# Float32r scores over stacked rows for the forgetting attention, with its forget sums moved into masks that GpSimd builds

## The chip, the cores and the metric

The kernel runs on one core of one Trainium2 chip. The metric is the device time of one execution in microseconds; the kernel before took 1037.12 us (median of 3 runs, 1036.83 to 1037.17). Engines are named as in the profile: PE is TensorE (PEld its weight loads), DVE is VectorE, ACT is ScalarE, POOL is GpSimd, SP is SyncE, which issues most of the DMAs. An engine works through its own instructions in the order in which they were written; they meet other engines through semaphores.

## What is computed

Two layers of a decoder trunk on 256 tokens of width 1024, all in float32. A layer is a half-step SwiGLU, a mixer and a second half-step SwiGLU, each behind an RMSNorm and added to the trunk. The mixer makes one projection `u @ w_in` and splits it into three groups of heads of width 64: A (4 query heads, one shared key head, keys chosen by a top-k indexer), B (4 heads, with 256 tokens plain causal attention), and C, the forgetting attention that the change is about:

```python
cq = rms_norm(cq, c_q_norm);  ck = rms_norm(ck, c_k_norm)          # 8 heads
log_f = log_sigmoid(cf + forget_bias);  c = cumsum(log_f)          # one value per token and head
s = einsum('bqhd,bkhd->bhqk', q, k) * D ** -0.5
s = s + c[query] - c[key]                                          # forget sums
s = where(key <= query, s, -inf);  p = softmax(s)
o_c = (p @ v) * sigmoid(cg)
h = h + concat(o_A, o_B, o_C) @ w_out
```

## The kernel before

**Tiling.** Tokens are two halves of 128 (`t` = 0, 1). Weights stream in as raw tiles of up to 1 MB (`Weights`, lines 57 to 139; SP issues the loads, five raw buffers). Each unit of 128 x 1024 numbers is split into a high part in float32r (a cast on ScalarE, line 118) and a low part (a subtraction on VectorE, line 122), and products are made of three float32r matmuls, high x high, high x low, low x high (`mm3`, line 305). `W.pump()` splits one more unit; it may run up to seven units ahead of the one in use, and the low part of a unit is made one pump after its high part. All matmuls but transposes go through `mm` (line 302), so they all stand at line 303 in the profile. A plain float32 matmul shows as two instructions there, a float32r one as one.

**The mixer's order.** `mixer` (line 660) walks the eight column groups of the projection in the order of `CHUNKS` (iq, ib, b, a, ck, cq, cv, cg), with four units each: 32 steps. After a step `run_side` (line 667) emits what `at_step(n, fn)` has put down for it, and then a pump follows. When a group is complete its `post_...` function takes the result out of PSUM. The side work that matters here: `log_sigmoid` at step 27; `cumsum` at step 29 (line 869), which sums the forget gates over tokens with two small matmuls and writes `c` and `-c`; `c_norm` at step 25 (line 977), which computes the RMS factors of the C queries and keys and scales both on GpSimd; `amask` at step 32; and `post_cg` after it (line 990), which makes the output gate `sg` of group C on ScalarE and VectorE.

**C queries and keys.** `cqa[t]` and `cka[t]` (lines 293 and 294) hold 8 heads of 66 columns: 64 of the head, then `c` and 1 for the queries, 1 and `-c` for the keys. So a product over 66 rows gives the score with the forget sums in it. `c_T(j)` (line 1135) turns two heads: four transposes of the queries, four of the keys, one copy on ScalarE, one on VectorE. `scores` (line 1004) then makes the C scores with two plain float32 matmuls a head (lines 1010 and 1011). Heads of A and B instead go through `products` (line 743): the query rows are stacked, 64 high over 64 low (`stack`, line 713), the keys stand twice, and two float32r matmuls, with the keys' high part and with their low part, do the work of a float32 one.

**The head loop** (lines 1149 to 1182) runs the 4 A heads and 8 C heads two at a time, in six blocks, software-pipelined. Block k emits: `flip` of the pair 2k, 2k+1 (transposes of the exponentials, line 1034), `outT` of the pair before (line 1064), `scores` of the next pair (one fused VectorE instruction for each half adds the mask, negates and takes the row minimum, line 1023), their exponentials (`exps`, line 1027), `c_T(k)` while k < 4, `values` of the pair (line 1043), and one or two halves of the output projection (`out_halves`, line 1120), whose every second half carries a pump. Ahead of the loop stand the scores and exponentials of the first pair and two halves. PSUM has four banks for the tag "gu", which all of these use in turn.

## Time and profile before

| | |
|---|---|
| median of 3 runs | 1037.12 us (1036.83 to 1037.17) |
| the profiled execution | 1037.25 us |
| its span, first to last instruction | 1035.5 us |
| granted TensorE clock | 1.000 |
| moved by DMA | 181.61 MB, mean 175 GB/s |

The prediction quotes views of the profile of that one execution. Shares of busy time by engine are an average over the span. The chain that ended last follows the work back from the last instruction: at each step to what released it. The timeline lists instructions in order of time; behind an instruction stands, in brackets, the idle time of its engine before it and what ended it. Groups by line give output, inputs, shapes, count, then busy time in us, mean ns of one, and the engine's idle time before them. A row of the DMA issues gives the size in KB and the median time from issue to landing in us. Ends of matmuls are modelled by the profiler, so a row's own length is longer than the distance from one matmul to the next.

### The profile page before, as it was taken

The page shows a single profiled execution, that of the slowest core. Times are in us where ns is not written, and L with a number is a line of the kernel's source. Part 1 is how long each engine was busy: PE and PEld are TensorE (multiplying, and loading weights), DVE is VectorE, ACT ScalarE, POOL GpSimd, SP SyncE. Part 2 cuts the span into 40 slices and gives each one's busy share as a digit, 9 for nine tenths or more (in the row PEclk, how much of TensorE's full clock was granted, in tenths as well). Part 3 has the DMA queues.
Part 4 walks back from the last instruction along what each step waited for, and adds up shares of the span by engine and source line. Part 5 has one row for each costly group of instructions (what it writes and reads, how often), then busy time and mean ns, then how long its engine had stood idle before and what let it go on. Part 6 is the DMA issues. An engine that isn't in the chain of part 4 may idle for free.

```text
span 1035.5 us, 15082 instructions
## 1 busy us (share of the span) xinstructions
PE 1031.3 (100%) x5641; PEld 898.4 (87%) x5641; DVE 808.0 (78%) x1537; ACT 592.1 (57%) x1045; POOL 147.3 (14%) x177
## 2 busy tenths in 40 slices
PE   9999999999999999999999999999999999999998
PEld 8888888898888888888888888888988988888887
DVE  6977778789876877777788777787898768777776
ACT  6655556666854655555465555557676646555552
POOL 2003000167800000000000110002766000000000
PEclk9999999999999999999999999999999999999999
DMA  9664656554431364645645564664455224564631
GB/s 324 224 240 162 208 188 198 182 191 170 158 127 42 123 230 150 230 168 203 198 163 193 182 224 146 241 186 172 164 195 170 83 69 160 180 204 162 236 130 41
DMA packets 130808, 181.61 MB, mean 175 GB/s; under 512 B 7040, under 2 KB 104624, under 8 KB 130736
## 3 DMA queue, kind: packets, MB, share of 16 engines
q1 hardware_dynamic: 130704, 180.66, 51.3%
q8 instruction: 44, 0.72, 0.3%
q14 instruction: 28, 0.23, 0.1%
q10 hardware_dynamic: 32, 0.01, 0.0%
HBM read 179.60 MB, written 1.05 MB: 174 GB/s over the span
## 4 chain that ended last, share of the span: by engine, by line
PE 100%; DVE 0%; POOL 0%; issue 0%; POOLq 0%
PE ps_gu L303 66%; PE ps_acc L303 30%; PE ps_acc L338 1%; PE ps_gu L1037 1%; PE ps_gu L1140 1%; PE ps_acc L738 0%; PE ps_acc L1037 0%; PE ps_gu L1070 0%; PE ps_acc L495 0%; PE ps_acc L364 0%; PE ps_acc L1070 0%; PE ps_gu L179 0%; DVE trunk L377 0%; POOL ones L183 0%; POOL minus_half L185 0%
## 5 line engine op out<-in xcount | busy, mean ns | idle before, releaser
L122 DVE TENSOR_TENSOR wl<-raw,wh 128x1024 fp32r<-128x1024 f32 (+2 forms) x342 | 417.0, 1225 | 24.7 <-ACT wh L118 24.7
L118 ACT CAST wh<-raw 128x1024 fp32r<-128x1024 f32 (+2 forms) x341 | 343.1, 1036 | 5.4 <-PE ps_gu L303 4.8
L303 PE MATMUL ps_gu<-xhl,wh 128*128 128x512 f32 x1408 | 330.2, 390 | 0.0
L303 PEld LDWEIGHTS ps_gu<-xhl,wh 128*128 128x128 f32 x1408 | 262.7, 188 | 53.8 <-ACT wh L118 0.3
L303 PEld LDWEIGHTS ps_gu<-xhl,wl 128*128 128x128 f32 x1408 | 176.0, 191 | 4.3 <-issue 0.2
L303 PE MATMUL ps_gu<-xhl,wl 128*128 128x256 f32 x1408 | 179.2, 283 | 0.1
L303 PE MATMUL ps_gu<-wh,xhl 128*128 128x512 f32 (+2 forms) x512 | 157.2, 377 | 0.0
L442 DVE TENSOR_TENSOR tmp<-ps_gu,tmp 128x256 f32<-128x256 f32 x176 | 73.0, 423 | 107.8 <-ACT tmp L441 107.5
L303 PE MATMUL ps_acc<-wh,hh 128*128 128x512 f32 (+1 forms) x352 | 137.2, 390 | 0.0
L303 PE MATMUL ps_acc<-wl,hh 128*128 128x512 f32 (+1 forms) x352 | 137.0, 389 | 0.0
L303 PE MATMUL ps_acc<-wh,hl 128*128 128x512 f32 (+1 forms) x352 | 136.5, 388 | 0.0
L441 ACT COPY tmp<-ps_gu 128x256 f32<-128x256 f32 x176 | 63.5, 371 | 93.5 <-PE ps_gu L303 93.2
L303 PEld LDWEIGHTS ps_gu<-wh,xhl 128*128 128x128 f32 x512 | 94.8, 188 | 14.6
L456 ACT CAST hh<-tmp 128x256 fp32r<-128x256 f32 x80 | 32.6, 407 | 119.7 <-DVE tmp L453 119.7
L303 PE MATMUL ps_gu<-wl,xhl 128*128 128x512 f32 (+2 forms) x256 | 95.7, 374 | 0.0
L448 ACT ACTIVATE tmp<-tmp 128x256 f32<-128x256 f32 x88 | 36.9, 419 | 82.3 <-DVE tmp L446 81.9
L314 POOL TENSOR_TENSOR y_n<-msq,minus_half 128x2 f32<-128x2 f32 x6 | 6.8, 1141 | 530.9 <-DVE msq L313 530.9
L303 PEld LDWEIGHTS ps_acc<-wh,hl 128*128 128x128 f32 x352 | 66.1, 188 | 13.9
L303 PEld LDWEIGHTS ps_acc<-wh,hh 128*128 128x128 f32 x352 | 66.2, 188 | 12.6
L303 PEld LDWEIGHTS ps_acc<-wl,hh 128*128 128x128 f32 x352 | 66.2, 188 | 12.2
L303 PEld LDWEIGHTS ps_gu<-wl,xhl 128*128 128x128 f32 x256 | 48.2, 188 | 6.7
L327 ACT ACTIVATE xhl<-ps_acc,gT 128x256 fp32r<-128x256 f32 x48 | 19.1, 474 | 38.7 <-PE ps_acc L338 35.6
(221 smaller groups left out, 1000.4 us busy)
## 6 DMA issues: line engine op xcount, KB each, us to landing
raw<-in_ffn_w_down_dram SPq DMA_DIRECT2D x44, 1024.0 KB, 4.9
raw<-in_ffn_w_gate_dram SPq DMA_DIRECT2D x42, 1024.0 KB, 6.6
raw<-in_ffn_w_up_dram SPq DMA_DIRECT2D x42, 1024.0 KB, 7.3
raw<-in_w_in_dram SPq DMA_DIRECT2D x24, 1024.0 KB, 4.9
raw<-in_w_out_dram SPq DMA_DIRECT2D x8, 1024.0 KB, 4.9
raw<-in_w_in_dram SPq DMA_DIRECT2D x4, 768.0 KB, 4.9
raw<-in_w_in_dram SPq DMA_DIRECT2D x4, 656.0 KB, 3.9
raw<-in_ffn_w_gate_dram SPq DMA_DIRECT2D x3, 512.0 KB, 7.0
```

Source lines behind the costliest of these rows:

```text
L118: self.nc.scalar.copy(hv, src)
L122: (engine or self.nc.vector).tensor_tensor(lv, self.srcs[self.n_low], hv.bitcast(F32), op=ALU.subtract)
L303: T.matmul(o, l, r, start=start, stop=stop, skip_group_check=True)
L314: G.tensor_tensor(y, dst, minus_half[:, :n], op=ALU.pow)
L327: A.activation(self.h[:, m], src, AF.Copy, scale=gT[:, self.col + m:self.col + m + 1])
L338: T.transpose(ps[:, i, t * P:(t + 1) * P], trunk[:, t, (2 * mp + i) * P:(2 * mp + i + 1) * P], ident)
L441: A.copy(o, ps[:, 1])
L442: V.tensor_tensor(o, ps[:, 0], o, op=ALU.add)
L448: A.activation(th, t_, AF.Tanh, scale=0.5)
L456: (V.tensor_copy if late else A.copy)(hh, t_)
L1037: T.transpose(b[:, j * P:(j + 1) * P], pj[i][:, j * P:(j + 1) * P], ident)
L1140: T.transpose(b[:66, i * S + t * P:i * S + (t + 1) * P], src[t][:, 2 * hp_ + i, :], ident)
```

## The change

The C heads get the form of A and B, and the forget sums leave the product.

- `cq` and `ck` (64 columns a head) take the place of `cqa` and `cka`; the memsets of their ones go. `c_norm` scales the queries only.
- `cumsum` keeps one copy of `c`. `turn_sums` (step 30) transposes `c` to rows by head with two transposes, negates it on ScalarE, and writes it to a scratch tensor in DRAM from ScalarE's queue; `load_sums` (step 31) reads it back from the same queue, broadcast over all 128 partitions (1 MB), into `minus_c`.
- `c_parts(j)` makes the stacked queries of two heads (high copy on ScalarE, low subtraction on GpSimd) and the doubled, scaled keys (two multiplications on GpSimd). Those of pairs 0 and 1 stand at step 31, those of pairs 2 and 3 at the end of blocks 1 and 2.
- `decay(j)` builds the masks of two heads on GpSimd in four additions: `-c[key]` + `c[query]` + causal mask. It stands ahead of the loop for pair 0 and at the end of blocks 0 to 2 for the others.
- `c_T(j)` turns queries with four float32r matmuls against the identity and keys with four transposes, then copies both on ScalarE; the keys' low part, a subtraction on VectorE (`key_low`), comes after the values of the block. The two buffers of `cT` alternate.
- The C scores go through `products`, and the fused VectorE instruction reads the head's mask.
- In the loop `exps(2k+2)` stands ahead of `c_T(k)` and `exps(2k+3)` behind it.

```diff
@@ cumsum, in post_ib
-                for t in range(2):
-                    c = b[:, 8 * t:8 * t + 8]
-                    A.copy(cqa[t][:, :, 64], c)
-                    A.activation(cka[t][:, :, 65], c, AF.Copy, scale=-1.0)
+                st["c"] = sm.tile([P, 2, 8], F32, name="c", tag="c", bufs=1)
+                A.copy(st["c"].rearrange("p t h -> p (t h)"), b[:, 0:16])
+
+            def turn_sums():
+                b = bank("acc")
+                for t in range(2):
+                    T.transpose(b[:8, t * P:(t + 1) * P], st["c"][:, t], ident)
+                n = tmp(S)[:8]
+                A.activation(n, b[:8, :S], AF.Copy, scale=-1.0)
+                st["row"] = dram.tile([8, S], F32, name="minus_c_row", tag="minus_c_row")
+                nc.scalar.dma_start(st["row"], n)
+
+            def load_sums():
+                d = st["row"]
+                st["minus_c"] = at.tile([P, 8, S], F32, name="minus_c", tag="kT")
+                nc.scalar.dma_start(st["minus_c"], bass.AP(tensor=d.tensor, offset=d.offset,
+                                                           ap=[[0, P], [S, 8], [1, S]]))
 
             at_step(SUMS_STEP, cumsum)
+            at_step(SUMS_STEP + 1, turn_sums)
+            at_step(SUMS_STEP + 2, load_sums)
@@ new functions
+        def c_parts(j):
+            hs2 = slice(2 * j, 2 * j + 2)
+            q = tp.tile([P, 512], F32R, name="stacked", tag="tmp")
+            q4 = q.rearrange("p (t h s d) -> p t h s d", t=2, h=2, s=2)
+            A.copy(q4[:, :, :, 0], cq[:, :, hs2])
+            G.tensor_tensor(q4[:, :, :, 1], cq[:, :, hs2], q4[:, :, :, 0].bitcast(F32), op=ALU.subtract)
+            k = tmp(512)
+            k4 = k.rearrange("p (t h s d) -> p t h s d", t=2, h=2, s=2)
+            for t in range(2):
+                G.tensor_tensor(k4[:, t], ck[:, t, hs2, None, :].to_broadcast([P, 2, 2, HD]),
+                                st["rk"][:, 8 * t + 2 * j:8 * t + 2 * j + 2, None, None].to_broadcast([P, 2, 2, HD]),
+                                op=ALU.mult)
+            beside[j] = [x.rearrange("p (t h c) -> p t h c", t=2, h=2) for x in (q, k)]
+
+        def decay(j):
+            m = st["minus_c"][:, 2 * j:2 * j + 2]
+            c = st["c"][:, :, 2 * j:2 * j + 2, None]
+            first = at.tile([P, 2, P], F32, name="first", tag="first", bufs=2)
+            tri2 = causal[:, None, 0:P].to_broadcast([P, 2, P])
+            G.tensor_tensor(first, m[:, :, 0:P], c[:, 0].to_broadcast([P, 2, P]), op=ALU.add)
+            G.tensor_tensor(first, first, tri2, op=ALU.add)
+            G.tensor_tensor(m, m, c[:, 1].to_broadcast([P, 2, S]), op=ALU.add)
+            G.tensor_tensor(m[:, :, P:S], m[:, :, P:S], tri2, op=ALU.add)
+            for i in range(2):
+                decays[2 * j + i] = first[:, i], m[:, i]
@@ c_norm, in post_cq
                 rs = head_rs(c_ss.rearrange("p i t h -> p (i t h)"), 32, "c")
-                for t in range(2):
-                    for i, d in enumerate((cka, cqa)):
-                        x = d[t][:, :, 0:64]
-                        scale_heads(x, x, rs[:, 16 * i + 8 * t:16 * i + 8 * t + 8])
+                st["rk"] = rs[:, 0:16]
+                for t in range(2):
+                    scale_heads(cq[:, t], cq[:, t], rs[:, 16 + 8 * t:24 + 8 * t])
 
             at_step(25, c_norm)
+            at_step(31, lambda: c_parts(0))
+            at_step(31, lambda: c_parts(1))
@@ scores
+                products(b[:, 0:P], q[:, 0:P], [c[:, 0:P] for c in k], True, True)
+                products(b[:, P:3 * P], q[:, P:S], [c[:, 0:S] for c in k], False, True)
                 if kind == "C":
-                    mm(b[:, 0:P], q[:, 0:P], k[:, 0:P], True, True)
-                    mm(b[:, P:3 * P], q[:, P:S], k[:, 0:S], False, True)
+                    masks = decays.pop(h)
...
-                    V.tensor_tensor_reduce(s[:, c], b[:, c], mask[:, c], scale, 3e38, op0=ALU.add, op1=ALU.min,
+                    V.tensor_tensor_reduce(s[:, c], b[:, c], masks[t], scale, 3e38, op0=ALU.add, op1=ALU.min,
@@ c_T
+        cT = xp.tile([P, 2, 4, 2, S], F32R, name="cT", tag="xhl")
+
+        def c_T(j):
+            q, k = beside.pop(j)
+            d = cT[:, j % 2]
+            bq, bk = bank("gu"), bank("gu")
+            for i in range(2):
+                for t in range(2):
+                    mm(bq[:, i * S + t * P:i * S + (t + 1) * P], q[:, t, i], identr, i + t == 0, True)
+            for i in range(2):
+                for t in range(2):
+                    T.transpose(bk[:, i * S + t * P:i * S + (t + 1) * P], k[:, t, i], ident)
+            bq, bk = (b.rearrange("p (h s) -> p h s", h=2) for b in (bq, bk))
+            A.copy(d[:, 0], bq)
+            A.copy(d[:, 1], bk)
+
+            def key_low():
+                V.tensor_tensor(d[:, 2], bk, d[:, 1].bitcast(F32), op=ALU.subtract)
+
+            return key_low
@@ the head loop
+        decay(0)
         two(0, scores, exps)
...
                 scores(2 * k + 3)
-                two(k + 1, exps)
+                exps(2 * k + 2)
             if k < 4:
-                c_T(k)
+                key_low = c_T(k)
             if not last:
+                exps(2 * k + 3)
                 two(k, values)
+            if k < 4:
+                key_low()
+            if 0 < k < 3:
+                c_parts(k + 1)
+            if k < 3:
+                decay(k + 1)
             for _ in range(HALVES[k]):
                 next(halves)
```

More of the change, by code (lines that the diff above doesn't have):

```diff
@@ L292 @@
     identr = cp.tile([P, P], F32R, name="identr")
-    cqa = [at.tile([P, 8, 66], F32, name=f"cqa{t}", tag=f"cqa{t}") for t in range(2)]
-    cka = [at.tile([P, 8, 66], F32, name=f"cka{t}", tag=f"cka{t}") for t in range(2)]
+    cq = at.tile([P, 2, 8, HD], F32, name="cq", tag="cq")
+    ck = at.tile([P, 2, 8, HD], F32, name="ck", tag="ck")
     va = [at.tile([P, 13, 65], F32, name=f"va{t}", tag=f"va{t}") for t in range(2)]
     for t in range(2):
-        G.memset(cqa[t][:, :, 65:66], 1.0)
-        G.memset(cka[t][:, :, 64:65], 1.0)
         G.memset(va[t][:, :, 64:65], 1.0)
@@ L958, in c_sums @@
             for t in range(2):
-                evac(dst[t][:, :, 0:64], heads(ps[t], 8), t)
+                evac(dst[:, t], heads(ps[t], 8), t)
                 sq.append(squares(ps[t], t, 8))
@@ L968, in post_ck @@
         def post_ck(ps):
-            c_sums(0, cka, ps, 21)
+            c_sums(0, ck, ps, 21)
         def post_cq(ps):
-            c_sums(1, cqa, ps, 25)
+            c_sums(1, cq, ps, 25)
             for t in range(2):
-                q = cqa[t][:, :, 0:64]
+                q = cq[:, t]
                 G.tensor_tensor(q, q, gc[:, None, :].to_broadcast([P, 8, HD]), op=ALU.mult)
@@ L1130, in mixer @@
         halves = out_halves()
-        c_both = xp.tile([P, 2, 8, S], F32, name="cT", tag="xhl")
-        cT = [c_both[:, 0], c_both[:, 1]]
-        def c_T(hp_):
-            for d, src in zip(cT, (cqa, cka)):
-                b = bank("gu")
-                for i in range(2):
-                    for t in range(2):
-                        T.transpose(b[:66, i * S + t * P:i * S + (t + 1) * P], src[t][:, 2 * hp_ + i, :], ident)
-                (A.copy if src is cqa else V.tensor_copy)(d[:66, 2 * hp_:2 * hp_ + 2],
-                                                         b[:66].rearrange("p (a b) -> p a b", a=2))
+        cT = xp.tile([P, 2, 4, 2, S], F32R, name="cT", tag="xhl")
[15 more added lines that the diff above has]
+            return key_low
         def qk_ac(kind, h):
```

10 lines of the change are left out of this document (6 added, 4 removed).

## The prediction

> **What bounds the kernel now.** I read the page's first part (busy time by engine) and its fourth (the chain that ended last, shares by engine) first.
>
> ```profile
> PE 1031.3 (100%) x5641; PEld 898.4 (87%) x5641; DVE 808.0 (78%) x1537; ACT 592.1 (57%) x1045; POOL 147.3 (14%) x177
> ```
>
> ```profile
> PE 100%; DVE 0%; POOL 0%; issue 0%; POOLq 0%
> ```
>
> TensorE is busy for the whole span and the chain never leaves it. So whatever TensorE no longer issues is saved one for one, and whatever makes it wait is lost one for one; the other engines count only where they make it wait. The stage of the change is the attention of each layer. Next I read the chain in order of time there (layer 0: start, length, what, count of instructions).
>
> ```profile
> 280.90 9.22 PE ps_gu L303 x44
> 290.12 2.77 PE ps_acc L303 x12
> 292.89 0.77 PE ps_gu L1037 x6
> 293.66 0.92 PE ps_gu L303 x8
> 294.58 0.87 PE ps_gu L1140 x8
> 295.45 1.29 PE ps_gu L303 x12
> 296.74 1.45 PE ps_acc L303 x6
> 298.19 0.66 PE ps_gu L1037 x6
> 298.85 0.22 PE ps_gu L1070 x2
> 299.06 1.31 PE ps_gu L303 x8
> 300.38 0.87 PE ps_gu L1140 x8
> ```
>
> The first row is steps 30, 31 and 32 (36 projection matmuls) and the scores of two A heads (8 instructions); with 0.92 for the scores, as in the fourth row, a step is (9.22 - 0.92) / 3 = 2.77 us, and the steps end at 283.67, 286.43 and 289.20. Then comes one `out_halves` pair, and at 292.89 block 0 of the head loop: flips, scores of two A heads, `c_T(0)`, values, one half. Block 1 starts at 298.19, and 299.06 is its scores of two C heads. There is no gap in the loop, but the first flips take 0.77 against 0.66 in block 1: there TensorE already waits for the first exponentials, so the entry of the loop has no slack. Blocks 2 and 3 have flips, outT, C scores, `c_T`, values and one half: 0.66 + 0.22 + 1.31 + 0.87 + 1.29 + 1.45 = 5.80 us.
>
> **The change, TensorE first.** C scores: a plain float32 pair (K = 66) takes 1.31 us, a float32r pair over 128 rows, which A is already, 0.92. That is -0.39 for each of 4 pairs in 2 layers: **-3.1 us**. A float32r matmul after float32 work can pay for the switch: six matmuls of a half take 1.45 behind the values, twelve 2.77 behind float32r scores, so 1.45 - 2.77 / 2 = 0.07. The A scores at 293.66 show nothing of it behind flips. Bounds 0 to 0.07 for each C pair, I take 0.05: **+0.4**. `c_T` keeps 8 instructions; the four that turn the queries are now float32r matmuls with the identity, at most 0.92 / 8 = 0.115 each as in the A scores, against 0.87 / 8 = 0.109: +0.02 a pair, **+0.2**. `turn_sums` adds two transposes (0.66 / 6 = 0.11 each) and one more return to float32r (0.07): 0.3 a layer, **+0.6**. The cumsum matmuls stay. TensorE alone: **-1.9 us**, bounds -2.7 (no switch, no dearer query) to -1.8.
>
> **The entry of the loop.** ScalarE and VectorE over steps 30 to 32 (timeline: start, length, what, idle before and its releaser):
>
> ```profile
> 283.80 1.05 ACT L118 CAST wh<-raw 128x1024 fp32r<-128x1024 f32 x1 [0.60 <-PE ps_gu L303]
> 286.52 1.06 ACT L118 CAST wh<-raw 128x1024 fp32r<-128x1024 f32 x1 [1.67 <-PE ps_gu L303]
> 289.52 1.27 ACT L995 ACTIVATE sg<-ps_gu,hr 128x512 f32<-128x512 f32 x2 [1.94 <-DVE hr L992]
> ```
>
> ```profile
> 288.13 1.22 DVE L122 TENSOR_TENSOR wl<-raw,wh 128x1024 fp32r<-128x1024 f32 x1
> 289.27 0.16 DVE L992 TENSOR_SCALAR hr<-y_n 128x2 f32<-128x2 f32 x1
> ```
>
> These chains feed the first exponentials: high part of a weight unit (ScalarE) - its low part (VectorE, 288.13) - `hr` - the gate `sg` (ScalarE) - two gate operations, score rows (VectorE) - exponentials - flips. Prices of what is put in, from the groups by line, from the start of the execution (an issue on ScalarE's queue) and from the DMA issues (size, us to landing):
>
> ```profile
> L1141 DVE COPY cT<-ps_gu 66x512 f32<-66x512 f32 x8 | 5.5, 684 | 0.0
> ```
>
> ```profile
> L1141 ACT COPY cT<-ps_gu 66x512 f32<-66x512 f32 x8 | 4.5, 561 | 0.0
> ```
>
> ```profile
> L741 DVE TENSOR_TENSOR bkT<-ps_acc,bkT 128x512 fp32r<-128x512 f32 x4 | 2.6, 677 | 0.0
> ```
>
> ```profile
> L740 ACT CAST bkT<-ps_acc 128x512 fp32r<-128x512 f32 x4 | 2.2, 615 | 0.0
> ```
>
> ```profile
> L717 ACT CAST stacked<-bqr 128x256 fp32r<-128x256 f32 x4 | 1.5, 464 | 0.0
> ```
>
> ```profile
> 0.78 0.46 ACTq L175 DMA_DIRECT2D tmp<-in_ffn_norm_dram  x1
> ```
>
> ```profile
> raw<-in_w_in_dram SPq DMA_DIRECT2D x24, 1024.0 KB, 4.9
> ...
> out_dram<-trunk SPq DMA_DIRECT2D x2, 128.0 KB, 1.8
> ...
> gb<-in_c_k_norm_dram SPq DMA_DIRECT2D x2, 32.0 KB, 8.1
> ...
> tmp<-in_ffn_norm_dram ACTq DMA_DIRECT2D x1, 8.0 KB, 2.5
> ```
>
> At step 30 ScalarE must wait for the transposes (283.67 + 0.22, and about 0.2 to be seen), negate (no row; bounds 0.2 to 0.46 between a short activation and L717, I take 0.4), and issue the write: 284.5. Its high part of step 30 runs to about 286.0. At step 31 the load stands in ScalarE's queue and waits until the write has landed; the smallest write of the trace takes 1.8, the 8 KB transfer on this queue 2.5: 286.3 to 287.0, and 0.46 for the issue (nothing, if ScalarE does not stand still for it): about 286.8 to 287.5. **Queued behind that waiting load** are the two copies of `c_parts(0)` and `(1)` (0.46 each at most), the high parts of steps 31 and 32, then the gate. The high part of step 31, which ran at 283.80, starts at 287.5 to 288.4. Its low part stood at 288.13 and now starts at 288.6 to 289.5, 0.5 to 1.4 later; 0.3 of that is TensorE's own delay. So the gate loses 0.2 to 1.1, or nothing if the issue is free and the write quicker than any row; I take 0.4.
>
> On VectorE there is a second cost. Two low parts while GpSimd scales C keys and queries, two without it, and GpSimd's own side at the first place (timeline):
>
> ```profile
> 276.76 4.05 DVE L122 TENSOR_TENSOR wl<-raw,wh 128x1024 fp32r<-128x1024 f32 x2
> ```
>
> ```profile
> 282.62 2.35 DVE L122 TENSOR_TENSOR wl<-raw,wh 128x1024 fp32r<-128x1024 f32 x2
> ```
>
> ```profile
> 276.70 1.05 POOL L690 TENSOR_TENSOR cqa<-cqa,y_c 128x512 f32<-128x512 f32 x1
> 277.70 2.03 POOL L690 TENSOR_TENSOR cka<-cka,y_c 128x512 f32<-128x512 f32 x1
> ```
>
> So a low part beside GpSimd operations costs (4.05 - 2.35) / 2 = 0.85 more, and the GpSimd one up to 1.0 more (2.03 against 1.05). From about 287.3 GpSimd now runs six operations of `c_parts`, where it had nothing to do before; the low part of step 31 falls among them: 0 to 0.85, I take 0.6. Together **+1.0 a layer, +2.0 us**; bounds 0 to 2.0 a layer. It meets the flips with no cover.
>
> [...]
>
> **The loop.** The last exponential of block 1 and the last of its values on VectorE (timeline), and GpSimd's groups of 256 elements, slow and fast:
>
> ```profile
> 301.46 0.49 ACT L1031 ACTIVATE p<-tmp,nm 128x256 f32<-128x256 f32 x1
> ```
>
> ```profile
> 302.78 0.29 DVE L1062 TENSOR_TENSOR o<-ps_gu,ri 128x128 f32<-128x128 f32 x1
> ```
>
> ```profile
> L684 POOL TENSOR_TENSOR bkr<-bkr,tab 128x256 f32<-128x256 f32 x4 | 5.0, 1256 | 0.3
> ...
> L684 POOL TENSOR_TENSOR aqr<-aqr,tab 128x256 f32<-128x256 f32 x4 | 3.1, 765 | 0.3
> ```
>
> VectorE gives up a copy (0.68) and takes up a subtraction (0.68), moved behind the values: nothing, as long as it ends before the next block's second flip, which reuses that bank. In block 1 the values end at 302.54 on TensorE (298.19 and the five pieces behind it) and at 303.07 on VectorE, 0.53 later; with two C heads a little more, 0.7. So in a block of 5.4 (5.80 - 0.39) they end at 4.0 and 4.7, the subtraction at 5.4, and the flip comes at 5.4 + 0.33 = 5.75: cover 0.3. ScalarE gives up 0.56 and takes up 2 x 0.62 and 0.46, 1.1 us a block; the second head's exponentials come some 1.2 later, and their flip is at 5.75 while they end before 5: hidden. Masks: the row operation only reads another tile, nothing.
>
> GpSimd: 256 elements cost 0.77 in the fast group, 512 cost 1.05, so `c_parts` is 3 x 0.77 = 2.3 and `decay` 3 x 0.77 + 1.05 = 3.35. The 1 MB of negated sums is issued near 287 and lands after 4.9 (a weight load) to 8.1 (the slowest broadcast), 292 to 295; `decay(0)` ends by 298.5. The first C row needs scores that start at 299.06, and some 1.5 later after the entry's loss: hidden. The narrow place is `c_parts(3)`: its copy follows the last exponentials of block 2. In block 1 those ended at 301.95, 3.76 after its start; with two copies ahead of them it is 5.0 (3.76 + 1.24), with its own copy about 5.3 (copies in a row overlap a little). GpSimd's three operations then end at 5.3 + 2.3 = 7.6, and a low part among them makes it 8.4. The keys are turned in block 3 at 5.45 + 0.66 + 0.22 + 0.92 + 0.46 = 7.7. Between nothing and 0.7, I take 0.5; with 0.1 for a low part beside `decay(0)` that delays score rows in block 0, **+0.6 a layer, +1.2 us**. `c_parts(2)` has block 1's second half of weights as cover (1.4).
>
> What else moves costs nothing, with this cover: `c_norm` drops two scalings and `cumsum` three small copies, ahead of units that ScalarE splits several steps before TensorE uses them; the memsets stood at the start; weight loads on SP's queue wait for low parts that are at most 1 us later, with up to five loads under way; the extra 1 MB a layer stands beside 181 MB. Without that cover each would cost no more than its own 0.2 to 1 us.
>
> Sum: -1.9 + 2.0 + 1.2 = **+1.3 us**. The profiled execution took 1037.25 (span 1035.5 and 1.75 around it), 0.13 above the median of the runs: 1038.55 there, **1038.4** as a median.
>
> **The rivals.**
> - *GpSimd becomes the bound (slower).* Place: `c_parts(3)` and `decay(3)`. If 256 elements cost L684's mean of 1.26 rather than 0.77, and 512 cost 1.5 (between 1.05 and 2.03), `c_parts` is 3.8 and `decay` 5.3. `c_parts(3)` then ends at 5.3 + 3.8 = 9.1, 1.4 late, and `decay(3)` 5.3 after that, 14.4, where the score rows of block 4 want it at 2 x 5.45 + 1.7 + 1.4 = 14.0: 1.4 and 0.4 are 1.8 a layer instead of 0.5. It decides from about 0.9 per 256 elements (3 x 0.9 + 5.3 = 8.0). Time 1041; with every operation at its contended worst (1.8 and 2.0), past 1050. For: the group's mean. [...]
> - [...] If each of the low part and the two gate operations waits for a whole GpSimd operation (0.77 to 0.85), the entry costs 0.4 + 2.3 = 2.7 rather than 1.0: +3.4, so 1041.8; halfway 1040. [...]
> - *Everything is hidden (faster).* If the write is quicker than any row, ScalarE does not stand still for an issue and GpSimd's operations miss the low parts, only TensorE's -1.9 is left (-2.7 to -1.8): 1035.2, 1034.4 to 1035.3. Against: the entry already waits, 0.77 against 0.66.
> - *The sums land late.* They would have to take 11 us (287 to 298); the slowest row is 8.1. Small, and inside the first rival. That float32r over 128 rows does not run at 0.92 a pair is excluded by the A rows.
>
> **How the numbers follow.** A run of this kernel can be told from no change at about 0.2%, 2.07 us: 1035.05 and 1039.2. Forecast, up to 1039.2: 0.46. All hidden: 0.16, half of it under 1035.05. GpSimd the bound: 0.23. The port at the gate: 0.15. So faster 0.08, same 0.46 + 0.08 = 0.54, slower 0.38. The range 1035.0 to 1042.5 leaves out about 0.07 below and 0.12 above; the forecast's own is 1036.3 to 1039.2.
>
> **What would show it.** C pairs of 8 instructions in 0.92 to 1.0 in the chain; two transposes of the sums and a `DMA` wait on ScalarE between steps 30 and 31; the gate 0.5 to 1.5 later behind the projection's end and first flips of more than 0.77 or a wait ahead of them; GpSimd near 0.77 per 256 elements; a wait ahead of the key transposes of block 3 alone. I am wrong if ScalarE passes step 31 without a wait, if TensorE waits for GpSimd in blocks 1, 2 or 4, or if low parts beside GpSimd keep 1.22.

## The result, and the profile after

The changed kernel takes 1043.56 us (median of 6 executions, 1041.04 to 1047.07) against 1037.03 (median of 6, 1036.83 to 1037.42) for the kernel before: a ratio of 1.0064, with a 95% interval of 1.0053 to 1.0076. It is slower by 0.64%, above the range of the prediction. The six times stand in two groups: 1041.0 to 1041.9 with a granted TensorE clock of 0.999 to 1.000 over the whole span, and 1045.2 to 1047.1 with 0.995. So there are two things to explain. The profiled execution took 1041.46 us and belongs to the first group; its span is 1039.4 us, 3.9 more than before, and 2.06 us lie around it instead of 1.75.

The busy time by engine and the chain that ended last, from the page of the changed kernel:

```profile
PE 1030.8 (99%) x5645; PEld 896.8 (86%) x5645; DVE 812.9 (78%) x1537; ACT 598.2 (58%) x1057; POOL 191.9 (18%) x225
```

```profile
PE 97%; DVE 2%; DMA 0%; ACT 0%; issue 0%; POOL 0%; SPq 0%; ACTq 0%
```

TensorE is busy for 0.5 us less than before and yet the span is longer: 97% of the chain is TensorE's and 2% is VectorE's, where it was 100%. So TensorE waits somewhere. The waits of TensorE (engine, line, for what; us in total, times, longest):

```profile
PE ps_gu L1084 <- ACT p L1077: 2.8, 2, 2.1
PE ps_gu L302 <- POOL minus_half L186: 1.0, 1, 1.0
PE ps_gu L1084 <- ACT p L1078: 0.4, 2, 0.2
...
PE ps_gu L302 <- DVE pT L1086: 0.3, 1, 0.3
```

The second row stands at the start of the program and was there before as well. L1084 is `flip`: the first flips of the head loop wait for the first exponentials, 2.1 us in layer 0 and 0.6 in layer 1. To see why the exponentials are late, follow VectorE's row of operations. First before (timeline; start, length, what), then after, both in layer 0:

```profile
287.19 0.23 DVE L858 TENSOR_SCALAR amask<-score 128x128 f32<-128x128 f32 x1
287.33 0.49 DVE L860 SCALAR_TENSOR_TENSOR amask<-score,cst 128x128 f32<-128x128 f32 x2
287.86 0.36 DVE L862 TENSOR_SCALAR amask<-amask 128x384 f32<-128x384 f32 x1
```

```profile
284.59 0.61 DVE L850 MAX8 m<-score 128x8 f32<-128x128 f32 x2
...
285.77 1.22 DVE L122 TENSOR_TENSOR wl<-raw,wh 128x1024 fp32r<-128x1024 f32 x1
286.91 0.77 DVE L857 TENSOR_SCALAR amask<-score 128x128 f32<-128x128 f32 x1
287.60 1.33 DVE L859 SCALAR_TENSOR_TENSOR amask<-score,cst 128x128 f32<-128x128 f32 x2
288.96 0.78 DVE L861 TENSOR_SCALAR amask<-amask 128x384 f32<-128x384 f32 x1
289.67 1.63 DVE L122 TENSOR_TENSOR wl<-raw,wh 128x1024 fp32r<-128x1024 f32 x1
291.22 0.58 DVE L1039 TENSOR_SCALAR hr<-y_n 128x2 f32<-128x2 f32 x1
```

From the mask on (L857) every operation has grown by 0.4 us or more, whatever its size: the two of L859 went from 0.49 to 1.33 together, and `hr`, which works on 2 columns, from 0.16 to 0.58. GpSimd's operations in that stretch, in layer 0 and in layer 1 of the changed kernel:

```profile
286.30 1.29 POOL L979 TENSOR_TENSOR stacked<-cq,stacked 128x256 fp32r<-128x256 f32 x1 [7.73 <-ACT stacked L978]
287.55 1.23 POOL L983 TENSOR_TENSOR tmp<-ck,y_c 128x256 f32<-128x256 f32 x2
288.74 0.78 POOL L979 TENSOR_TENSOR stacked<-cq,stacked 128x256 fp32r<-128x256 f32 x1
289.49 2.27 POOL L983 TENSOR_TENSOR tmp<-ck,y_c 128x256 f32<-128x256 f32 x2
```

```profile
801.82 1.82 POOL L979 TENSOR_TENSOR stacked<-cq,stacked 128x256 fp32r<-128x256 f32 x1 [7.72 <-ACT stacked L978]
```

These are `c_parts(0)` and `c_parts(1)`. The ends of the two engines' operations alternate there: GpSimd's lie at 287.59, 288.16, 288.78, 289.52, 290.21 and 291.77, VectorE's, from the mask on, at 287.68, 288.31, 288.93, 289.74, 291.30 and 291.80. (Alone in the loop an operation of GpSimd's on 256 elements takes 0.61 to 0.75.) The two gate operations behind `hr` meet `decay(0)`, which begins at 292.41: 0.69 and 0.94 instead of 0.43 each. In layer 1 the first GpSimd operation took 1.82 instead of 1.29: there it was GpSimd's operation that grew, the mask's first three kept their lengths (0.22, and 0.48 together), and the loss was smaller. ScalarE did not stand still until the write had landed, as the prediction had it. Its timeline at steps 30 and 31:

```profile
284.13 0.51 ACTq L883 DMA_DIRECT2D minus_c_row<-tmp  x1
284.68 1.05 ACT L118 CAST wh<-raw 128x1024 fp32r<-128x1024 f32 x1 [0.58 <-ACT tmp L881]
285.43 0.35 ACTq L888 DMA_DIRECT2D minus_c<-minus_c_row  x1
285.82 0.71 ACT L978 CAST stacked<-cq 128x256 fp32r<-128x256 f32 x2
...
291.89 1.26 ACT L1042 ACTIVATE sg<-ps_gu,hr 128x512 f32<-128x512 f32 x2 [3.46 <-DVE hr L1039]
```

The load goes out 1.3 us after the write (284.13 and 285.43), while ScalarE works on its high part, so nothing on ScalarE stands still for the load; the write's own issue leaves 0.58 idle ahead of that high part. And ahead of the gate's tanh ScalarE waits 3.46 us for `hr` (1.94 before).

Where the time went is told by three stretches of TensorE's timeline in each layer, from the start of one instruction to the start of another: the **entry**, from the first matmul of `cumsum` (step 29) to the first flips of block 0; **block 0**, to the first flips of block 1; and **blocks 1 to 5**, to the first instruction of L337 behind the loop. Between the two layers' attention lie 460.02 or 460.03 us in every kernel; the start of the program varies by up to 1.0 from one profiled execution to the next. Layer 0 / layer 1, with the experiments that follow:

| kernel | time, us | entry | block 0 | blocks 1 to 5 |
|---|---|---|---|---|
| before | 1037.03 | 12.34 / 12.34 | 5.30 / 5.30 | 35.09 / 35.09 |
| after | 1043.56 | 14.84 / 13.34 | 6.30 / 6.49 | 34.35 / 34.06 |
| c0_after (again) | 1042.16 | 14.72 / 13.34 | 7.56 / 6.21 | 34.32 / 34.07 |
| e2_before_parts | 1041.00 | 13.29 / 13.46 | 6.01 / 6.00 | 35.07 / 35.06 |
| e14_before_sums | 1037.91 | 12.55 / 12.56 | 5.18 / 5.17 | 35.01 / 35.01 |
| e1_28 | 1043.93 | 14.40 / 13.81 | 6.88 / 6.56 | 34.32 / 34.08 |
| e8_load_32 | 1043.63 | 14.77 / 13.35 | 7.26 / 6.86 | 34.33 / 34.05 |
| e6_keys_act | 1040.13 | 13.06 / 13.06 | 6.86 / 6.39 | 34.31 / 34.09 |
| e9_29_load_32 | 1038.35 | 12.56 / 12.56 | 6.07 / 6.30 | 34.37 / 34.05 |
| e11_q29_keys_act | 1037.77 | 12.56 / 12.56 | 6.06 / 5.47 | 34.32 / 34.09 |
| e12_load_last | 1037.80 | 12.55 / 12.56 | 5.70 / 5.47 | 34.34 / 34.09 |
| e13_keys_split | 1036.80 | 12.55 / 12.55 | 5.24 / 5.24 | 34.35 / 34.09 |
| e4_filler | 1042.01 | 14.73 / 13.98 | 6.30 / 5.48 | 34.33 / 34.05 |
| e15_before_pause | 1044.08 | 14.41 / 14.39 | 6.01 / 6.00 | 35.06 / 35.10 |

After against before: the entries lose 2.50 and 1.00, block 0 loses 1.00 and 1.19, blocks 1 to 5 gain 0.74 and 1.03, and the start was 0.30 earlier; together +3.6 of the 3.9 us that the span grew.

### The profile page after: what moved, and what is told of

Its sections match the earlier page's. It is cut to its first block, busy times and chain, and to the rows that moved or that the text cites. A ratio compares the mean times of both kernels' runs of the same rounds, so it can differ in the third digit from the quotient of the medians.

```text
span 1039.4 us, 15190 instructions
## 1 busy us (share of the span) xinstructions
PE 1030.8 (99%) x5645; PEld 896.8 (86%) x5645; DVE 812.9 (78%) x1537; ACT 598.2 (58%) x1057; POOL 191.9 (18%) x225
## 3 DMA queue, kind: packets, MB, share of 16 engines
HBM read 181.70 MB, written 1.06 MB: 176 GB/s over the span
## 4 chain that ended last, share of the span: by engine, by line
PE 97%; DVE 2%; DMA 0%; ACT 0%; issue 0%; POOL 0%; SPq 0%; ACTq 0%
PE ps_gu L302 65%; PE ps_acc L302 29%; PE ps_acc L337 1%; DVE wl L122 1%; PE ps_gu L1084 1%; PE ps_gu L1190 0%; DMA raw<-in_ffn_w_gate_dram 0%; DVE sg L1044 0%; PE ps_acc L737 0%; PE ps_acc L1084 0%; PE ps_gu L1117 0%; DVE tmp L1070 0%; ACT sg L1042 0%; PE ps_acc L494 0%; DVE score L852 0%
```

## The experiments

Theory A: GpSimd's operations beside VectorE's short ones cost the entry, since VectorE's row there is what TensorE waits for. Theory B, of the prediction: a good part comes from ScalarE's queue with the sums' write and load. Theory C, for the second group of times: the pause of TensorE's at the head of the loop lets its clock fall. The kernel before took 1037.4 to 1037.6 on the chips of these executions.

**The parts without the sums, the sums without the parts.** The first edit adds to the kernel before operations like those of `c_parts(0)` and `(1)`, read by nobody:

```diff
+            def beside_it(j):
...
+                G.tensor_tensor(q4[:, :, :, 1], q4[:, :, :, 0].bitcast(F32), q4[:, :, :, 0].bitcast(F32), op=ALU.subtract)
+                for t in range(2):
+                    G.tensor_tensor(k4[:, t], cka[t][:, hs2, None, 0:64].to_broadcast([P, 2, 2, HD]), y, op=ALU.mult)
+            at_step(31, lambda: beside_it(0))
+            at_step(31, lambda: beside_it(1))
```

> The kernel before, with operations like those of c_parts(0) and c_parts(1) at step 31 (ScalarE's copies, GpSimd's six operations of 256 columns), whose results nobody reads: no new scores, no sums through memory, no gains in the loop. Theory A: the entry's loss appears alone, +3.5 and +2.2 us, so 1041 to 1043, and the upper group of times with a clock of 0.995 may come with it. Theory B: 1037.0 to 1038, since neither the write nor the load is there and ScalarE has 3.5 us to spare behind its copies.

Measured: 1041.00 us, ratio 1.0037 (1.0025 to 1.0050). Entry +0.95 and +1.12, block 0 +0.71 and +0.70, nothing in blocks 1 to 5. VectorE's timeline in this kernel:

```profile
286.48 1.61 DVE L122 TENSOR_TENSOR wl<-raw,wh 128x1024 fp32r<-128x1024 f32 x1
288.01 0.63 DVE L858 TENSOR_SCALAR amask<-score 128x128 f32<-128x128 f32 x1
288.56 1.34 DVE L860 SCALAR_TENSOR_TENSOR amask<-score,cst 128x128 f32<-128x128 f32 x2
289.94 0.36 DVE L862 TENSOR_SCALAR amask<-amask 128x384 f32<-128x384 f32 x1
```

The same growth of the low part and of three of the mask's four operations, without any other part of the change; here the six operations are over before the mask's last one and `hr`, which keep their 0.36 and 0.16. Entries and blocks 0 lose 3.5 us in all, of the 5.7 that they lose in the changed kernel. The second edit gives the kernel before `turn_sums` and `load_sums` as they are in the change, and nobody reads `minus_c`.

> The kernel before, with the sums turned, written to memory and loaded for 128 partitions as in the changed kernel, and nobody reading them: no GpSimd operation, no new scores. Theory B (the entry is late by ScalarE's queue with the write and the load, 0.4 us a layer as the prediction had it): 0.7 us more for the turning and 0.8 for the waits, 1038.5 to 1039. Theory A: only the turning on TensorE (0.2 us a layer in the runs that have it without waits) and what lies outside the span (0.35 us more in every kernel that writes the sums to memory than in the kernel before): 1037.8 to 1038.3, with no wait of TensorE's in either entry.

Measured: 1037.91, ratio 1.0004 (0.9995 to 1.0013). The entry is 0.21 longer, which is the turning on TensorE, and TensorE waits nowhere in it. ScalarE's timeline:

```profile
286.11 0.35 ACTq L894 DMA_DIRECT2D minus_c<-minus_c_row  x1
...
289.92 1.27 ACT L1016 ACTIVATE sg<-ps_gu,hr 128x512 f32<-128x512 f32 x2 [1.41 <-PE ps_gu L304]
```

The tanh starts 9.1 us behind `cumsum`, as before, though ScalarE is idle for 0.59 at the issue of the write. Theory B falls: neither the write nor the load makes the tanh later. The parts alone make 3.5 of the 5.7 us and the turning 0.4; the other 1.8 appear only with the whole change, where `decay(0)` runs beside the gate and beside a low part of block 0; no run takes these apart.

**Moving the parts.** If GpSimd's operations are the cost, they should be put where VectorE's row has room. GpSimd was idle for 7.7 us ahead of them, so the first attempt was to start them there:

```diff
-            at_step(31, lambda: c_parts(0))
-            at_step(31, lambda: c_parts(1))
+            at_step(28, lambda: c_parts(0))
+            at_step(28, lambda: c_parts(1))
```

> c_parts(0) and c_parts(1) at step 28 and not 31, nothing else changed: GpSimd does its six operations in the 7.7 us in which it was idle, and the mask of selected keys, the last low part and the gate run alone. Theory A (GpSimd's operations beside VectorE's short ones are the cost: entry +3.5 us in layer 0, +2.2 us in layer 1): most of both entries comes back, 1035 to 1036.5, one group of times. Theory B (the entry is late by ScalarE's queue with the sums' write and load, and by the turning of the sums): 1040.5 to 1042 as before. Third case (the same operations now hold up weight splits and the selection's rounds at steps 28 to 31, and the delay is handed on to the entry): 1038 to 1040.

Measured: 1043.93, ratio 1.0065 (1.0052 to 1.0079): a miss of theory A's number. ScalarE's and VectorE's timelines tell why:

```profile
278.98 0.71 ACT L978 CAST stacked<-cq 128x256 fp32r<-128x256 f32 x2 [1.00 <-POOL cq L689]
```

```profile
282.10 0.76 DVE L1128 TENSOR_TENSOR ol<-ps_acc,oh 128x256 fp32r<-128x256 f32 x2 [2.07 <-ACT oh L1124]
...
288.52 0.22 DVE L857 TENSOR_SCALAR amask<-score 128x128 f32<-128x128 f32 x1
288.66 0.48 DVE L859 SCALAR_TENSOR_TENSOR amask<-score,cst 128x128 f32<-128x128 f32 x2
...
290.59 0.58 DVE L1039 TENSOR_SCALAR hr<-y_n 128x2 f32<-128x2 f32 x1
291.99 2.12 DVE L1044 TENSOR_SCALAR sg<-sg 128x512 f32<-128x512 f32 x2 [0.82 <-ACT sg L1042]
```

The mask is back at 0.22 and 0.48, so the mechanism holds. But the copies now waited 1.00 us in ScalarE's queue for GpSimd's scaling, ahead of the evictions of `va` and of the last B outputs, and VectorE's row began 1.3 us later. And `decay(0)`, whose sums now find GpSimd free, runs beside the gate: 1.06 for a gate operation instead of 0.43. What was won in one place was lost in two others.

Four more experiments followed: the keys' multiplications of the two pairs on ScalarE, at step 32 (the loop's pairs 2 and 3 unchanged); the load of the sums a step later; `c_parts` at step 29, behind those evictions, with the later load; and all three moves:

```diff
+                        A.activation(k4[:, t, i], ck[:, t, h, None, :].to_broadcast([P, 2, HD]), AF.Copy,
+                                     scale=st["rk"][:, 8 * t + h:8 * t + h + 1])
...
+            at_step(32, lambda: c_keys(0))
+            at_step(32, lambda: c_keys(1))
```

> The keys' multiplications of c_parts(0) and c_parts(1) go from GpSimd to ScalarE, as eight scaled copies at step 32 in a stretch in which ScalarE waited 3.5 us for VectorE; GpSimd keeps two of six operations at step 31. Theory A (every GpSimd operation at the entry costs the VectorE operation beside it some 0.5 us, and VectorE's row of operations is what TensorE waits for): two thirds of the entry's loss comes back, about 2 us in layer 0 and 1 in layer 1, so 1038.5 to 1039.5. Theory B (the loss is in ScalarE's queue): more work on ScalarE ahead of the gate's tanh makes it worse, 1042 to 1044.

> Only the load of the sums is a step later (32), so decay(0) starts some 3 us later, behind the gate and the first score rows. Theory A: one gate operation of 0.87 us falls to 0.43 in layer 0 and perhaps one more, while a later low part meets decay(0) instead: 0.3 to 1 us less, 1040.5 to 1041.5. Theory B (the load's place in ScalarE's queue is the cost): a loss of 2 us or more comes back, below 1040. If decay(0) becomes late for the first C scores: 1043 or more, with a wait of TensorE's or VectorE's for minus_c in block 1.

> c_parts(0) and c_parts(1) at step 29, behind the evictions of va and of the last B outputs in ScalarE's queue (at step 28 the copies stood ahead of them and waited 1.0 us for GpSimd, which made VectorE's row start 1.3 us later), and the load of the sums at step 32. Theory A: the mask, the last low part and the gate run alone (3.2 us less), three low parts at steps 29 to 31 pay 0.4 to 0.8 us each, and the loop's gain of about 2 us shows: 1035.5 to 1038. Theory B, or a VectorE row that has no room at steps 29 to 31 either: 1040 to 1042.

> The three moves together: queries' parts at step 29, keys' multiplications on ScalarE at step 32, the load of the sums at step 32, so that GpSimd does two operations of 256 columns at steps 29 to 30 and none at the entry. Theory A: TensorE waits under 0.5 us in each entry and the loop's gain is left, 1035 to 1036.5, below the kernel before. Theory B, or keys on ScalarE that hold up the gate's tanh: 1038 to 1042.

Measured: 1040.13 (1.0027, 1.0016 to 1.0038), 1043.63 (1.0065, 1.0049 to 1.0080), 1038.35 (1.0009, 1.0000 to 1.0017) and 1037.77 (1.0005, 0.9997 to 1.0014). With two GpSimd operations at the entry instead of six it loses 0.72 in each layer instead of 2.50 and 1.00. With none it loses 0.22, the turning alone. The load a step later tested nothing: it went out 1.3 us behind the write and 5.3 us behind `cumsum`, as in the changed kernel, so this was the changed kernel once more. All four times lie above what theory A gave, by 0.6, 2.1, 0.4 and 1.3 us: block 0 kept a loss of its own (6.06 to 7.26 in layer 0 instead of 5.30). With `c_parts` at step 29 GpSimd works beside low parts and selection rounds; in VectorE's timeline of that kernel two low parts cost 0.5 more together than the 2.35 that the prediction quotes, the selection rounds nothing:

```profile
282.85 2.82 DVE L122 TENSOR_TENSOR wl<-raw,wh 128x1024 fp32r<-128x1024 f32 x2
285.59 0.61 DVE L850 MAX8 m<-score 128x8 f32<-128x128 f32 x2
```

The kernel with all three moves was forecast below the kernel before and is not, since block 0 of layer 0 still takes 6.06, and of layer 1 5.47. The difference is one low part, here in layer 0 and in layer 1:

```profile
293.18 1.56 DVE L122 TENSOR_TENSOR wl<-raw,wh 128x1024 fp32r<-128x1024 f32 x1
...
805.90 1.22 DVE L122 TENSOR_TENSOR wl<-raw,wh 128x1024 fp32r<-128x1024 f32 x1
```

In layer 0 `decay(0)` began at 293.05, just ahead of it; in layer 1 at 806.41, behind it. So the load of the sums was put behind the keys' copies in the program (both at 31.9), and then, with that kept, the copies of pair 0 into a wait of ScalarE's for the turned sums (at 29.9, as here):

```diff
-            at_step(32, lambda: c_keys(0))
-            at_step(32, lambda: c_keys(1))
+            at_step(29.9, lambda: c_keys(0))
+            at_step(31.9, lambda: c_keys(1))
```

> The kernel of the three moves, with the load of the sums behind the eight keys' copies in ScalarE's queue: it is issued some 3 us later, lands near 296 us in layer 0, and decay(0) starts behind the low part of block 0 and not beside it. In the run before, that low part took 1.56 us in layer 0, where decay(0) had begun 0.1 us ahead of it, and 1.22 us in layer 1, where decay(0) began 0.5 us behind it; block 0 took 6.06 and 5.47 us. Theory A: block 0 of layer 0 falls to some 5.5 us, so 0.4 to 0.6 us less than that kernel, 1037.0 to 1037.5. If decay(0) becomes late for the first C scores: block 1 longer than 6.9 us, and no gain.

> As the kernel with the load last, but the four keys' copies of pair 0 stand at step 29.9, in a wait of 1.35 us that ScalarE had for the turned sums, and only those of pair 1 behind step 31. Theory A (what is left at the entry is ScalarE's 2.4 us of keys ahead of the last high part and the gate's tanh): the same 1037.0 to 1037.5 or 0.2 less, with ScalarE waiting for VectorE again ahead of the tanh. Rival (step 30's turning of the sums and the high part behind it come later and hold up VectorE's row): 1037.5 to 1038.5.

Measured: 1037.80 (1.0003, 0.9994 to 1.0012) and 1036.80 (0.9994, 0.9985 to 1.0003), against 1037.42 for the kernel before. The first edit did not do what it was to do. In ScalarE's timeline of that kernel the load goes out ahead of the eight copies, which stand ahead of it in the program:

```profile
285.75 0.35 ACTq L888 DMA_DIRECT2D minus_c<-minus_c_row  x1
...
286.90 2.46 ACT L992 ACTIVATE tmp<-ck,y_c 128x128 f32<-128x128 f32 x8
```

In every profile with the write and the load, wherever the load stands in the program, it goes out 1.3 us behind the write, so this issue did not keep its place in the program. So this was the kernel of the three moves again, and its time is the same. Block 0 of layer 0 fell by 0.36 because the load happened to land 0.24 us later, so that `decay(0)` began just behind the start of the low part, which kept 1.22. The second edit did move something: without the copies of pair 0 ahead of it the gate's tanh starts 9.3 us behind `cumsum` instead of 9.8, and block 0 takes 5.24 in both layers. Its waits of TensorE:

```profile
PE ps_gu L302 <- POOL minus_half L186: 1.0, 1, 1.0
PE ps_acc L494 <- DMA trunk<-in_x_dram: 0.2, 1, 0.2
```

Both stand at the start of the program; this view lists no wait in either layer's attention (some of 0.2 us are left, see below). This version is 5 to 7 us faster than the changed kernel and 0.6 us below the kernel before, where the interval still includes no difference.

**The second group of times.** The changed kernel once more:

> The changed kernel again, for a second profile and more times. Its six times so far stand in two groups, 1041.0 to 1041.9 at a granted clock of 0.999 to 1.000 and 1045.2 to 1047.1 at 0.995. Theory C (TensorE's pause of 2.1 us at the head of the loop lets the clock fall in some executions): both groups come again, and a profile that falls in the upper one shows a window with a granted clock below 1.00 right behind one of the pauses, worth 4 to 6 us. Rival (the two groups are a matter of the run, not of the pause): the low clock stands somewhere else, or is spread over the span.

Measured: 1042.16 (1.0042, 1.0029 to 1.0054), one execution of five at 0.998 and none at 0.995, so the upper group did not come again. The profiled execution was that of 0.998. TensorE in stretches around the head of the loop in layer 0 (us; length, busy time and count; granted clock; DMA share; GB/s):

```profile
293.00:295.20 2.20, 0.24 (x2) 1.00 0.97 307
295.20:296.60 1.40, 1.09 (x5) 1.00 0.71 252
296.60:298.10 1.50, 1.50 (x10) 0.66 0.00 0
298.10:299.80 1.70, 1.70 (x11) 0.50 0.00 0
299.80:301.40 1.60, 1.60 (x14) 0.78 0.00 0
301.40:302.80 1.40, 1.40 (x8) 1.00 0.00 0
```

The first row is the pause. Behind it and the six flips the granted clock falls to 0.50 and comes back. An estimate from these rows, with 0.50 (the fourth row's clock) for the whole of the fall: the shortfalls, (0.34 x 1.5 + 0.50 x 1.7 + 0.22 x 1.6) / 0.5, make 3.4 us at half clock. Block 0 took 7.56 us instead of 6.30. The load that tested nothing (e8_load_32) shows the same again in layer 0, also 3.4 us by the same sum:

```profile
295.30:296.70 1.40, 1.22 (x5) 0.70 0.64 225
296.70:298.10 1.40, 1.40 (x9) 0.50 0.00 0
298.10:299.60 1.50, 1.50 (x10) 0.61 0.00 0
```

Two experiments ask for the cause. One fills the pause, with matmuls that nobody reads:

```diff
+        b = bank("gu")
+        for i in range(12):
+            mm(b[:, :S], identr, st["akT"][:, 0, 0], i == 0, i == 11)
         for k in range(n):
```

> The changed kernel with twelve float32r matmuls of 256 columns, into a bank that nobody reads, between the first two heads' scores and their flips: TensorE works through some 1.5 us of the 2.1 us in which it waited there in layer 0, and is held up by some 0.5 to 1 us in layer 1, where it waited for 1.1 in three pieces. Theory C (the pause lets the clock fall): the group at 0.995 is gone, all times from 1041.5 to 1042.5, so the median falls by about 1. Rival (the groups have nothing to do with the pause): two groups again, each 0.5 to 1 us higher, median 1044 or so.

Measured: 1042.01 (1.0043, 1.0031 to 1.0056), 1041.64 to 1042.62, all five at a clock of 1.000. The other makes the pause in the kernel before, with nothing of the change:

```diff
+            x = tmp(512)
+            for _ in range(6):
+                V.tensor_scalar(x, sg[:, 1], 0.5, 0.5, op0=ALU.mult, op1=ALU.add)
             st["sg"] = sg
```

> The kernel before with six more gate operations of 512 columns on VectorE (0.43 us each, into a tile that nobody reads) behind the gate, so that TensorE waits some 2.0 to 2.6 us ahead of the first flips in both layers, with no GpSimd operation, no sums in memory and no new scores. Theory C (a pause of TensorE's of about 2 us there, whatever its cause, lets the clock fall for some microseconds in some executions): entry of 14.3 to 15.0 us in both layers, 1041.5 to 1042.5 where the clock stays, and several executions at 0.995 to 0.999 with 1 to 5 us more, in a profile such a stretch at a granted clock of 0.75 to 0.8 right behind a pause. Rival (the low clock came with GpSimd's operations, the sums or the float32r work): every execution at 1.000 within 0.5 us of the others, 1041.5 to 1042.5.

Measured: 1044.08 (1.0066, 1.0053 to 1.0078), 1042.72 to 1045.77; three of six executions at 0.997 to 0.998, and those are the three slowest. The other three, at 1.000, took 1042.7 to 1043.8, above both forecasts, since block 0 lost 0.7 a layer besides the pause. TensorE's waits:

```profile
PE ps_gu L1040 <- ACT p L1033: 3.8, 2, 1.9
```

The profiled execution was one at 1.000, so no row of this kernel shows the fall itself; the clocks of the executions do. Over all kernels, executions with a clock below 0.999 against the longest wait of the first flips:

| first flips waited, us | executions below 0.999 |
|---|---|
| 1.7 to 2.1, and not filled (after, c0, e1, e8, e15) | 14 of 28 |
| 0.8 to 1.0 (e2) | 1 of 5 |
| 0.3 to 0.5 (e4, e6) | 0 of 11 |
| none (e9, e11, e12, e13, e14) | 0 of 55 |

Theory C holds: the low clock comes with the pause, whatever makes it, and none of the 66 executions in which it was filled, short or gone shows a clock below 0.999. What stays open is why 6 of the 28 (of after, e1 and e8) fell to 0.995 and the others to 0.997 or 0.998. By an estimate from c0_after, where a stretch of 3.4 us at 0.50 loses 1.7, that is about three such stretches (0.005 x 1040 = 5.2) and one or two; none of the six was profiled.

## Why the prediction was wrong

- **TensorE bounds the kernel, and the entry has no slack.** Right: 0.1 us of a wait at the first flips had been the only sign of it, and what entries and blocks 0 lost and the loop gained makes up 3.6 of the 3.9 us of the span.
- **TensorE alone, -1.9 us.** The direction is right, the size is off. Without any long wait (e13_keys_split) the three stretches change by +0.21 and +0.21, -0.06 and -0.06, -0.74 and -1.00: -1.4. The turning costs 0.4, not 0.6. The loop gives -1.9, not -2.5. The chain in order of time (start, length, what, count): first block 4 of layer 0 in the kernel before, 8 instructions of scores and 12 of values, then in e13_keys_split the keys' transposes of blocks 0 and 1 in layer 0, and block 4 of layer 1:

```profile
317.85 2.60 PE ps_gu L303 x20
```

```profile
295.87 0.46 PE ps_gu L1204 x4
...
301.25 0.63 PE ps_gu L1204 x4
...
830.30 2.21 PE ps_gu L302 x20
```

  In block 4 of layer 1 the scores save 0.39, the whole price of a pair, with nothing for a change of number format, for which 0.05 a pair was put down. In block 0 the turned queries and keys take 0.87 as before (0.41 and 0.46), so a change costs next to nothing there too. What took the rest of the gain are short waits, for which the prediction had no term. In blocks 1 to 3 the scores, `c_T` and their gaps save only 0.16 to 0.23 in place of 0.39: the keys' transposes, or in block 3 the second head's scores, start some 0.2 us late, and in block 2 of the changed kernel the first weight load of the transposes shows 0.19 us of idle time. The profile names a GpSimd operation for that one, but the keys had been ready for 1.6 us, so what it waited for is open. In block 4 of layer 0, TensorE loses another 0.26.
- **The entry, +1.0 a layer.** This is the step that failed. Its part on **ScalarE's queue** (0.4) is zero: the load went out 1.3 us behind the write, below every landing time in the sum, and ScalarE passes step 31 without a wait, which the prediction named as a sign that it is wrong. The 0.2 put down for ScalarE to see the transposes is in no row that the prediction quotes; the negation began 0.03 behind their modelled end (283.69 and 283.72). Its part on **VectorE** (0.6) counted one low part among GpSimd's operations. In its place every one of eight VectorE operations paid 0.3 to 0.5 us: four of the mask, the low part and `hr` beside `c_parts`, two gate operations beside `decay(0)`, 3.4 together in layer 0. The entry lost 2.50 in layer 0, above the bound of 2.0 even without the 0.2 of the turning; the 1.00 of layer 1 is near the number put down by luck, since none of it came from ScalarE's queue. The mask's four operations, next to that low part in VectorE's row and as near to GpSimd's six, were in no term of the sum.
- **The rival of 1041.8**, in which the low part and the two gate operations each wait for a whole GpSimd operation, named the right place, with 2.7 us for the entry; the first executions at full clock took 1041.0 to 1041.9. It got a chance of 0.15. That the gate operations wait was the author's supposition: no row that the prediction quotes has one beside GpSimd, and the port that its chance names is shown by no run; what the runs show is which operations grew, and by how much. It named the low part and the gate; the mask, which goes the same way, it did not. That its number fits is partly luck: its 0.4 of ScalarE's queue was zero, it charged three operations 0.77 where eight paid about 0.4, and 2.2 of the 5.7 us were lost in blocks 0, which it left out. Not everything on VectorE grew beside GpSimd: the low part, the mask's four operations (L857, L859, L861), `hr` and the gate did, by 0.3 to 0.5 each in the entry of layer 0; MAX8 kept 0.61 (e9_29_load_32), and the row operations on the scores took 0.34 and 0.47 beside `decay(0)` (294.09 to 295.51 in the changed kernel), against 0.35 and 0.48 before.
- **The loop, +0.6 a layer.** Wrong in its place: `c_parts(3)` was not late: its keys were ready at 316.01 and turned from 316.24 on, and blocks 1 to 5 gain 0.72 to 0.78 in layer 0 and 1.00 to 1.04 in layer 1 in every kernel with the new loop. But block 0, for which 0.1 was put down, lost 1.00 and 1.19: late exponentials of the first two heads there, and a low part and copies beside `decay(0)`. **The rival "GpSimd becomes the bound"** is refuted: in the loop 256 elements took 0.61 to 0.75 and 512 took 1.04, except for operations beside a low part (1.59 to 1.71, and 2.02 for 512).
- **The clock.** No part of the prediction had it. The executions of the changed kernel that show it are longer, by 1.2 us in c0_after (1042.84 at 0.998 against a median of 1041.65 for its other four) and by 4.7 in the first six (medians of 1046.14 at 0.995 and 1041.46). The seven executions of the changed kernel at 0.999 or 1.000 took 1040.7 to 1042.7 us, above the forecast too, all but one inside its range; the clock brought the median of the first six to 1043.6.

## What to carry to other kernels

Before work is put on an idle GpSimd, list the VectorE operations that will run beside it, and charge those of the kinds that grew here, however small, what they paid here, 0.3 to 0.5 us each beside GpSimd operations of 0.6 to 0.75 (alone): their ends alternated, and a row of eight operations lost 3.4 us where the forecast had charged one long one 0.6. Where a unit of work moves, move with it what it waits for: the same six operations cost the entry of layer 0 2.3 us at step 31, 1.9 at step 28, where a copy ahead of them waited in another engine's queue, and nothing at step 29. An edit that moves an instruction in the program need not move it on the chip: see where it ran before its time is read as an answer. And a pause of TensorE's can cost more than its own length: after pauses of 1.7 to 2.1 us 14 of 28 executions here had a clock below 0.999, and in both profiles that caught the fall the clock behind the pause went down to 0.50, for 3.4 us by the estimate above.

## What the runs showed of the hardware that was not expected

- A write to DRAM and a load of it from the same queue of ScalarE's, issued 1.3 us apart, made TensorE wait nowhere in the entry (e14_before_sums), and ScalarE was idle only for 0.59 us at the issue of the write; the 1 MB of the load landed 7.3 us after its issue (median in the changed kernel). The load kept these 1.3 us (1.29 to 1.32 in eleven profiles) also where eight copies of 2.46 us in all stood ahead of it in the program.
- The half clock (0.50) was profiled twice, in c0_after and e8_load_32, behind pauses of TensorE's of 2.0 and 2.1 us followed by six transposes, and lasted 3.4 us by the estimate above each time; of the executions with a pause of 1.7 to 2.1 us, 14 of 28 had a clock below 0.999.
- Every kernel with the sums in its masks spends 2.03 to 2.21 us outside the span, the kernel before 1.67 to 1.79. The sums' write and load alone give 1.69 to 2.16 in eleven executions, and the parts alone 1.74 to 2.00 in five, so neither is the whole of it; what makes these 0.35 us is open.
- Layer 0's blocks 1 to 5 take 0.2 to 0.3 us longer than layer 1's in every kernel with the new loop, and not before. The time is lost in block 4: there, in the changed kernel, VectorE's second row operation on the first head's scores starts 0.19 us behind the end of the first (321.36 to 321.55), where in layer 1 it starts before that end (835.47 and 835.54), and TensorE's second head's values start behind it. What holds VectorE up there is open.
